# Forgetting attention: logits as three passes over keys and queries split in two parts

## The chip, the cores and the metric

The kernel runs on one core of one Trainium2 chip. The metric is the device time of one execution in microseconds; where several runs are shown it is their median. The profile is of one execution, taken by the hardware profiler, and has its own time.

## The reference, cut to what matters

One layer of a decoder trunk: x is 512 tokens of width 2048, 16 learned tokens go ahead of them, and everything is in float32. One projection makes the inputs of three mixers that work side by side on their own heads: a gated DeltaNet (6 heads of 128), a gated linear attention (5 heads), and the forgetting attention (5 heads of 128) that this document is about. Their outputs, each times a SiLU gate, go through one output projection.

```python
def forgetting_attention(q, k, v, log_f):
    c = jnp.cumsum(log_f, axis=-1)
    ...
    def one_block(args):          # swept in blocks of 128 queries
        i, q_i, c_i = args
        q_pos = i * BLOCK + jnp.arange(BLOCK)
        logits = jnp.einsum('bhqd,bhkd->bhqk', q_i, k) + c_i[..., :, None] - c[:, :, None, :]
        mask = (key_pos[None, :] <= q_pos[:, None]) & (key_pos[None, :] >= PAD)
        probs = jax.nn.softmax(jnp.where(mask, logits, NEG), axis=-1)
        return jnp.einsum('bhqk,bhkd->bhqd', probs, v)
    ...

def hybrid_layer(x, ...):
    proj = (h @ w_in).astype(f32)
    ...
    log_f = jax.nn.log_sigmoid(ff + b_f.astype(f32)).transpose(0, 2, 1)
    o_fox = forgetting_attention(to_heads(fq, FOX_HEADS) * FOX_D ** -0.5, to_heads(fk, FOX_HEADS),
                                 to_heads(fv, FOX_HEADS), log_f)
    o_fox = o_fox.reshape(fz.shape) * jax.nn.silu(fz)
    o = jnp.concatenate([o_dn, o_gla, o_fox], axis=-1)[:, PAD:].astype(x.dtype)
    return x + o @ w_out
```

## The kernel before

Everything is held transposed: 128 columns of a head on the partitions, the T = 528 positions (16 learned tokens, then 512) along the free axis.

**The input projection.** `inproj` makes one block of 128 output columns at a time. The weights come in halves of 128x1024 (`load_half`); each half is split into a high part `hi`, a copy in the type float32r, and a low part `lo`, the rest (L149 on ScalarE, L150 on VectorE). The input is split in the same way into `xh` and `xl`. For each of 16 slices of the contraction L198 issues three passes, hi·xh, hi·xl and lo·xh, into one PSUM bank of 512 columns, or into two of 264 where the 16 learned tokens are wanted too. A product of such split parts is one instruction on TensorE, a product of two float32 tensors is two. The output projection (L992) works in the same three passes.

**A head of the forgetting attention** (`fox_head`). The projections of keys, values, queries and gate are evacuated from PSUM by `evac`, which multiplies by the norm's factor (L316, and L318 for queries, which are scaled too). Keys and queries are float32 and lie in one tile of three rows of 528 columns, `qk`, of which the middle row is unused. Values and probabilities are split into high and low parts; the fourth block of both also has a float32 copy.

Per block b of 128 queries the logits are two products in full precision, with the queries of the block as weights: `pfa` (L903) against the 16 + 128 b positions before the block, `pfd` (L904) against the block itself. So `pfa` has 16, 144, 272 and 400 columns, and `pfd` always 128. VectorE subtracts the forget bias and takes the maximum of each row (L907, L909), ScalarE takes the exponential (L912), VectorE divides by the sum (L913 to L917). TensorE transposes the probabilities (L920, into `pfx`), which are split again (L923, L924). After the fourth block the outputs are accumulated (L936 to L939) and multiplied by the gate (L940).

```python
        for b in range(NB):
            m = NM + b * P
            ts = bsl(b)
            ...
            PE.matmul(pa[:, :m], qT[:, ts], kT[:, :m], start=True, stop=True)
            PE.matmul(pd[:, :P], qT[:, ts], kT[:, ts], start=True, stop=True)
```

**What sets the order.** A scheduler lays out each engine's instructions when the program is built; on the chip every engine takes its own in that order. Between a block's logits and its transposes stand some 50 matmuls of the next projections (of the output projection in the last head), which fill TensorE while softmax runs on VectorE and ScalarE. Buffers that matter here: the pool tag `row` has seven buffers of 128x531 for values, probabilities, gates and the like; `six` has eight of 128x1584 (the tile `qk` is one); the PSUM tag `m` has four banks, shared by logits, transposes and outputs. Loads of weights are issued by SyncE.

Of the kernel before, what the change touches and what calls it, by code (L numbers as in the profile page):

```python
# [8 lines left out]
F32 = mybir.dt.float32  # L9
F32R = mybir.dt.float32r  # L10
# [4 lines left out]
ALU = mybir.AluOpType  # L15
# [3 lines left out]
P = 128  # L19
D = 2048  # L20
KT = D // P
NM = 16
S = 512
T = NM + S
# [53 lines left out]
def tile_hybrid_trunk(ctx, tc, xT, xtok, mtok, w_gate, w_in, w_out, consts, lmask, fin_w, out, dbg=None):  # L78
# [8 lines left out]
    six = pool("six", 8)  # L87
    wk = pool("wk", 2)
# [4 lines left out]
    def row(name, dt=F32):  # L93
        return wk.tile([P, 3 + T], dt, tag="row", bufs=7, name=name)
# [4 lines left out]
    V, A, G, PE = nc.vector, nc.scalar, nc.gpsimd, nc.tensor  # L99
# [93 lines left out]
    def inproj_part(ps, parts, k0, n, hi, lo, m=P):  # L193
        for j in range(n):
            k = k0 + j
            for wt, xx in ((hi, xh), (hi, xl), (lo, xh)):
                for p_, (t0, nt) in zip(ps, parts):
                    mm = PE.matmul(p_[:, :nt], wt[:, j * m : (j + 1) * m], xx[k][:, t0 : t0 + nt],  # L198
                                   start=(k == 0 and wt is hi and xx is xh),
                                   stop=(k == KT - 1 and wt is lo))  # L200
                    order.append(mm.ins)

    def inproj_begin(key, meta=True, first=0):
        b = BLOCK_OF[key]
        n = (T - first) // 2
        parts = [(first, n), (first + n, n)] if meta else [(NM, S)]
        ps = [psb.tile([P, 512], F32, tag="b", name=f"pp{b}_{i}") for i in range(len(parts))]
        return b, ps, parts
# [3 lines left out]
    def inproj(key, meta=True, first=0):  # L212
        if key not in done:
            b, ps, parts = inproj_begin(key, meta, first)
            head[key] = len(order)
            for half in range(2):
                inproj_part(ps, parts, 8 * half, 8, *load_half(w_in[b, half], f"{b}_{half}"))
            done[key] = [(p_[:, :n], t0, n) for p_, (t0, n) in zip(ps, parts)]
        return done.pop(key)
# [91 lines left out]
    def evac(parts, dst, off=0, rows=slice(0, P), scale=None):  # L311

        for p_, t0, n in parts:
            o = dst[rows, off + t0 : off + t0 + n]
            if scale is None:
                V.tensor_tensor(out=o, in0=p_[rows], in1=rstd[rows, t0 : t0 + n], op=ALU.mult)  # L316
            else:
                V.scalar_tensor_tensor(out=o, in0=p_[rows], scalar=scale, in1=rstd[rows, t0 : t0 + n],  # L318
                                       op0=ALU.mult, op1=ALU.mult)
# [29 lines left out]
    for k in range(KT):  # L349
        for xx in (xh, xl):  # L350
            for a in range(2):
                PE.matmul(pgate[a][:, :HT], wg[k // 8][:, k % 8, :], xx[k][:, a * HT : (a + 1) * HT],  # L352
                          start=(k == 0 and xx is xh), stop=(k == KT - 1 and xx is xl))
# [505 lines left out]


    def fox_head(h):
        qk = six.tile([P, 3, T], F32, tag="six", name=f"fqk{h}")
        kT, qT = qk[:, 0], qk[:, 2]
        evac(inproj(("fk", h)), kT)

        v = row(f"vf{h}")[:, :T]
        evac(inproj(("fv", h)), v)
        pv = psm.tile([P, 512], F32, tag="m", name=f"pvf{h}")
        for b in range(NB):
            PE.transpose(pv[:, b * P : (b + 1) * P], v[:, bsl(b)], ident)  # L870
        vhi, vlo = (row(f"v{n}{h}", dt=F32R)[:, :S] for n in ("hi", "lo"))
        v3 = t15(f"v3{h}", (P, P))
        A.copy(vhi, pv)
        V.tensor_tensor(out=vlo, in0=pv, in1=vhi.bitcast(F32), op=ALU.subtract)
        A.copy(v3, pv[:, 3 * P :])
        v4 = t15(f"v4{h}", (P, 2 * NB, NM))
        G.tensor_copy(v4, v[:, 0:NM].unsqueeze(1).to_broadcast([P, 2 * NB, NM]))
        pw = psm.tile([P, 512], F32, tag="m", name=f"pwf{h}")
        PE.transpose(pw[:, :P], v4.rearrange("p b t -> p (b t)"), ident)
        vm = t15(f"fvm{h}", (P, 2, P), F32R)  # L880
        A.copy(vm[:, 0], pw[:, :P])
        V.tensor_tensor(out=vm[:, 1], in0=pw[:, :P], in1=vm[:, 0].bitcast(F32), op=ALU.subtract)
        evac(inproj(("fq", h), meta=False), qT, scale=float(P) ** -0.5)
        cc = six.tile([P, 2 * T + S], F32, tag="six", name=f"fc{h}")
        z = wk.tile([P, S], F32, tag="gd", name=f"fz{h}") if h < 2 else cc[:, T + S : T + 2 * S]
        gate_z("fz", h, z)
        cb, cm = cc[:, :T], cc[:, T : T + S].rearrange("p (b t) -> p b t", b=NB)
        nc.scalar.dma_start(out=cb, in_=gd[12 + h, :].partition_broadcast(P))
        G.affine_select(out=cm, in_=cb[:, NM:].rearrange("p (b t) -> p b t", b=NB), pattern=[[0, NB], [-1, P]],
                        base=0, channel_multiplier=1, compare_op=ALU.is_ge, fill=BIG)  # L890


        mt = t15(f"fmt{h}", (P, NB, 2, NM), F32R)
        pm = row(f"ptm{h}", dt=F32R)[:, :S]
        G.tensor_copy(pm, zero_c.to_broadcast([P, S]))
        hi, lo = (six.tile([P, 3, T], F32R, tag="six", name=f"fp{n}{h}") for n in ("hi", "lo"))
        p3 = t15(f"fp3{h}", (P, P))
        for b in range(NB):
            m = NM + b * P
            ts = bsl(b)  # L900
            pa = psm.tile([P, 512], F32, tag="m", name=f"pfa{h}{b}")
            pd = psm.tile([P, 512], F32, tag="m", name=f"pfd{h}{b}")
            PE.matmul(pa[:, :m], qT[:, ts], kT[:, :m], start=True, stop=True)  # L903
            PE.matmul(pd[:, :P], qT[:, ts], kT[:, ts], start=True, stop=True)  # L904
            pr = row(f"fp{h}{b}")[:, :T]
            sm = wk.tile([P, 4], F32, tag="fsm", name=f"fsm{h}{b}")
            V.tensor_tensor_reduce(out=pr[:, :m], in0=pa[:, :m], in1=cb[:, :m], scale=1.0, scalar=-3e38,  # L907
                                   op0=ALU.subtract, op1=ALU.max, accum_out=sm[:, 0:1])
            V.tensor_tensor_reduce(out=pr[:, m : m + P], in0=pd[:, :P], in1=cm[:, b], scale=1.0, scalar=sm[:, 0:1],  # L909
                                   op0=ALU.subtract, op1=ALU.max, accum_out=sm[:, 1:2])  # L910
            V.tensor_scalar_mul(sm[:, 2:3], sm[:, 1:2], -1.0)
            A.activation(pr[:, : m + P], pr[:, : m + P], AF.Exp, bias=sm[:, 2:3], accum_out=sm[:, 3:4])  # L912
            V.reciprocal(sm[:, 0:1], sm[:, 3:4])  # L913
            V.tensor_scalar_mul(mt[:, b, 0], pr[:, :NM], sm[:, 0:1])
            V.scalar_tensor_tensor(out=mt[:, b, 1], in0=pr[:, :NM], scalar=sm[:, 0:1],
                                   in1=mt[:, b, 0].bitcast(F32), op0=ALU.mult, op1=ALU.subtract)
            V.tensor_scalar_mul(pr[:, NM : m + P], pr[:, NM : m + P], sm[:, 0:1])  # L917
            px = psm.tile([P, 512], F32, tag="m", name=f"pfx{h}{b}")
            for jb in range(b + 1):
                PE.transpose(px[:, jb * P : (jb + 1) * P], pr[:, NM + jb * P : NM + (jb + 1) * P], ident)  # L920
            n = min(b + 1, 3)
            x, bs = px[:, : n * P].rearrange("p (j t) -> p j t", j=n), slice(b * P, (b + 1) * P)
            A.copy(hi[:, :n, bs], x)  # L923
            V.tensor_tensor(out=lo[:, :n, bs], in0=x, in1=hi[:, :n, bs].bitcast(F32), op=ALU.subtract)  # L924
            if b == 3:
                A.copy(p3, px[:, 3 * P :])
        pw = psm.tile([P, 512], F32, tag="m", name=f"pfw{h}")
        PE.transpose(pw[:, :P], mt.bitcast(F32).rearrange("p b i t -> p (b i t)"), ident)
        for b in range(NB):
            r, bs = slice(32 * b, 32 * b + 32), slice(b * P, (b + 1) * P)  # L930
            A.copy(pm[r, bs], pw[r, :P])
        po = psm.tile([P, 512], F32, tag="m", name=f"pfo{h}")
        for jb in range(3):
            js, qs = slice(jb * P, (jb + 1) * P), slice(jb * P, S)
            for i, (v_, p_) in enumerate(((vhi, hi), (vhi, lo), (vlo, hi))):
                PE.matmul(po[:, qs], v_[:, js], p_[:, jb, qs], start=(jb + i == 0), stop=False)  # L936
        PE.matmul(po[:, 3 * P :], v3, p3, start=False, stop=False)
        for i in range(2):
            PE.matmul(po, vm[:, i], pm, start=False, stop=i == 1)  # L939
        V.tensor_tensor(out=z, in0=po[:, :512], in1=z, op=ALU.mult)  # L940
# [89 lines left out]
    for cc in range(4):  # L1030
# [6 lines left out]
        pa = [psb.tile([P, 512], F32, tag="b", name=f"pa{cc}{tb}") for tb in range(4)]  # L1037
# [20 lines left out]
    for c in range(4):  # L1058
        f = part(f"fw{c}").bitcast(F32)
# [86 lines left out]
```

## Time and profile before

| what | value |
|---|---|
| median of 3 runs | 1019.95 us (1019.50 to 1020.04) |
| the profiled execution's own time | 1018.81 us |
| its span, first to last instruction | 1017.1 us |
| mean granted TensorE clock | 0.998 |
| TensorE busy | 1006.3 us, 99% |
| VectorE busy | 558.2 us, 55% |
| ScalarE busy | 416.5 us, 41% |
| GpSimd busy | 135.5 us, 13% |

PE is TensorE's matmuls, PEld its loads of weights, DVE VectorE, ACT ScalarE, POOL GpSimd, SP SyncE. A row of the order of time has the start and the length in us, the engine, the line, the operation, what is written from what, the shape (weights, then the moving operand) and how many instructions in a row are merged. Matmuls overlap, so their lengths do not add up; from start to start they do. A row of grouped instructions has the count, then busy time in us, the mean length of one in ns, and the engine's idle time ahead of them with what ended it. A row of waits has the total in us, how many, and the longest. Both types of operand, float32 and its split parts, are shown as f32 in matmul rows.

### The profile page before, as it was taken

What the parts mean: (1) busy time and instruction counts of PE and PEld (TensorE: products, weight loads), DVE (VectorE), ACT (ScalarE), POOL (GpSimd) and SP (SyncE); (2) the same over time, 40 slices, a digit from 0 to 9 for tenths busy, and PEclk for the clock granted to TensorE, in tenths of its full rate; (3) what the DMA queues carried; (4) which work ended last, traced back from release to release, by engine and by line L of the source; (5) the groups of instructions that cost most, each with busy time, mean ns of one, the idle gap of its engine ahead of it and who ended that gap; (6) DMA issues with size and microseconds to landing.
All of it is one profiled execution on the core that took longest, in us unless ns stands there. A gap on an engine that the chain in (4) does not pass through costs nothing.

```text
span 1017.1 us, 18766 instructions
## 1 busy us (share of the span) xinstructions
PE 1006.3 (99%) x7662; PEld 907.4 (89%) x7662; DVE 558.2 (55%) x1226; ACT 416.5 (41%) x916; POOL 135.5 (13%) x141
## 2 busy tenths in 40 slices
PE   9999999999999999999999999999999999999996
PEld 8899999899999888998999979898989888888885
DVE  6376867856566984343838373544444474323333
ACT  7653533443456333344544434333333362223224
POOL 0021411211112221100110021010101000000014
PEclk9999999999999999999999999999999999999999
DMA  9623133233221333222122222322223263232244
GB/s 356 221 68 131 65 99 105 83 100 104 91 79 64 98 104 100 71 79 70 63 65 69 67 92 63 94 92 70 92 82 92 85 204 128 83 104 90 96 145 166
DMA packets 42410, 105.03 MB, mean 103 GB/s; under 512 B 10733, under 2 KB 13981, under 8 KB 42324
## 3 DMA queue, kind: packets, MB, share of 16 engines
q1 hardware_dynamic: 28064, 92.23, 27.3%
q10 hardware_dynamic: 14260, 11.61, 4.1%
q8 instruction: 60, 0.98, 0.4%
q14 instruction: 26, 0.21, 0.1%
HBM read 98.64 MB, written 5.05 MB: 102 GB/s over the span
## 4 chain that ended last, share of the span: by engine, by line
PE 92%; DVE 3%; ACT 2%; DMA 1%; POOL 1%; issue 1%; ACTq 1%; DVEq 0%; POOLq 0%
PE pp L198 57%; PE pa L992 16%; PE pp L252 4%; PE pss L773 1%; POOL stgz L325 1%; PE pgate L352 1%; PE pfo L936 1%; PE pfa L903 1%; DVE ot L507 1%; DVE wlo L150 1%; PE pg L474 1%; PE pa L615 1%; PE py L639 1%; DMA sc<-ab 1%; PE pb L992 1%
## 5 line engine op out<-in xcount | busy, mean ns | idle before, releaser
L198 PE MATMUL pp<-xl,whi 128*128 128x264 f32 (+2 forms) x1456 | 378.6, 310 | 0.0
L198 PE MATMUL pp<-xh,whi 128*128 128x264 f32 (+2 forms) x1456 | 376.1, 310 | 0.1
L198 PE MATMUL pp<-xh,wlo 128*128 128x264 f32 (+2 forms) x1456 | 375.2, 309 | 0.4 <-DVE wlo L150 0.4
L198 PEld LDWEIGHTS pp<-xl,whi 128*128 128x128 f32 x1456 | 244.4, 189 | 13.6 <-issue 0.2
L198 PEld LDWEIGHTS pp<-xh,wlo 128*128 128x128 f32 x1456 | 243.6, 188 | 14.2 <-DVE wlo L150 0.9
L198 PEld LDWEIGHTS pp<-xh,whi 128*128 128x128 f32 x1456 | 243.0, 188 | 14.5 <-issue 0.8
L149 ACT CAST whi<-raw 128x1024 fp32r<-128x1024 f32 x110 | 115.4, 1049 | 201.5 <-PE pp L198 159.8
L150 DVE TENSOR_TENSOR wlo<-raw,whi 128x1024 fp32r<-128x1024 f32 x110 | 134.6, 1224 | 108.5 <-ACT whi L149 98.2
L992 PE MATMUL pa<-whio,ol 128*128 128x512 f32 x224 | 88.1, 393 | 0.0
L992 PE MATMUL pa<-wloo,oh 128*128 128x512 f32 x224 | 88.0, 393 | 0.0
L150 DVE TENSOR_TENSOR wloo<-rawo,whio 128x1024 fp32r<-128x1024 f32 x29 | 35.9, 1236 | 81.2 <-ACT whio L149 81.2
L992 PE MATMUL pa<-whio,oh 128*128 128x512 f32 x224 | 78.0, 396 | 0.0
L149 ACT CAST whio<-rawo 128x1024 fp32r<-128x1024 f32 x29 | 30.4, 1050 | 83.7 <-PE pa L992 65.1
L992 PEld LDWEIGHTS pa<-whio,ol 128*128 128x128 f32 x224 | 42.1, 188 | 9.8
L992 PEld LDWEIGHTS pa<-wloo,oh 128*128 128x128 f32 x224 | 42.1, 188 | 9.4
L992 PEld LDWEIGHTS pa<-whio,oh 128*128 128x128 f32 x224 | 41.9, 188 | 9.2
L325 POOL TENSOR_SCALAR stc<-cv 128x528 f32<-128x528 f32 (+1 forms) x18 | 28.2, 1564 | 138.3 <-DVE cv L409 115.3
L409 DVE SCALAR_TENSOR_TENSOR cv<-pb,cpk,cv 128x528 f32<-128x528 f32 (+1 forms) x54 | 40.8, 755 | 0.7
L1019 POOL TENSOR_TENSOR acc<-acc,fw 128x512 f32<-128x512 f32 x12 | 15.7, 1349 | 159.1 <-DMA fw<-in_fin_w 159.1
L316 DVE TENSOR_TENSOR pb<-pp,rstd 128x264 f32<-128x264 f32 (+1 forms) x36 | 13.7, 422 | 23.3 <-PE pp L198 23.3
L507 DVE TENSOR_TENSOR ot<-ab 51x30 f32<-51x30 f32 (+14 forms) x60 | 21.2, 354 | 3.6 <-DMA ab<-scmeta 2.1
L325 POOL TENSOR_SCALAR stfz<-zfz 128x512 f32<-128x512 f32 x5 | 9.8, 1965 | 99.0 <-ACT whi L149 49.0
(391 smaller groups left out, 1285.4 us busy)
## 6 DMA issues: line engine op xcount, KB each, us to landing
raw<-in_w_in SPq DMA_DIRECT2D x110, 512.0 KB, 3.3
rawo<-in_w_out SPq DMA_DIRECT2D x29, 512.0 KB, 3.3
xt<-in_xtok SPq DMA_DIRECT2D x8, 512.0 KB, 9.8
acc<-in_xtok ACTq DMA_DIRECT2D x16, 256.0 KB, 5.1
out<-acc SPq DMA_DIRECT2D x16, 256.0 KB, 3.0
xs<-in_xT SPq DMA_DIRECT2D x7, 528.0 KB, 6.7
gb<-gd ACTq DMA_DIRECT2D x2, 792.0 KB, 6.1
eg<-gd ACTq DMA_DIRECT2D x8, 192.0 KB, 3.4
```

The source lines that it names most:

```text
L149: A.copy(hi, raw)
L150: V.tensor_tensor(out=lo, in0=raw, in1=hi.bitcast(F32), op=ALU.subtract)
L198: mm = PE.matmul(p_[:, :nt], wt[:, j * m : (j + 1) * m], xx[k][:, t0 : t0 + nt], start=(k == 0 and wt is hi and xx is xh), stop=(k == KT - ...
L252: mm = PE.matmul(ps[:, :S], wt[:, j * P : (j + 1) * P], xx[k][:, NM:T], start=(k == 0 and wt is hi and xx is xh), stop=(k == KT - 1 and wt ...
L316: V.tensor_tensor(out=o, in0=p_[rows], in1=rstd[rows, t0 : t0 + n], op=ALU.mult)
L325: G.tensor_scalar_max(t, src, LOW)
L352: PE.matmul(pgate[a][:, :HT], wg[k // 8][:, k % 8, :], xx[k][:, a * HT : (a + 1) * HT], start=(k == 0 and xx is xh), stop=(k == KT - 1 and ...
L409: V.scalar_tensor_tensor(out=c, in0=pb[:, t0 + w : w + T], scalar=cwc[:, blk, w : w + 1], in1=c, op0=ALU.mult, op1=ALU.add)
L474: PE.matmul(pg[:r, j * r : (j + 1) * r], kT[:, j, ts], kT[:, j, ts], start=True, stop=True)
L507: V.tensor_tensor(out=t3, in0=a3[:, j + 1 :, j : j + 1].to_broadcast([NN * 4 + H, m, j]), in1=a3[:, j : j + 1, 0:j].to_broadcast([NN * 4 + ...
L992: PE.matmul(p_, o_[:, s], w_, start=(first and n == 0), stop=(last and n == 2), **kw)
L1019: G.tensor_tensor(out=acc[tb, cc], in0=acc[tb, cc], in1=fw[cc], op=ALU.mult)
```

## The change

Keys and queries are each written first into a float32 buffer `kf` of which there is one, shared by both. From there ScalarE copies the high part in float32r and VectorE makes the low part. High and low keys and high queries take the three rows of `qk`; the queries' low part takes a `row` buffer. Each of the two products of a block becomes three passes accumulated in PSUM: high queries with high keys, high queries with low keys, low queries with high keys; the passes of `pfa` and `pfd` alternate. The product of the two low parts is left out.

```diff
     def fox_head(h):
-        qk = six.tile([P, 3, T], F32, tag="six", name=f"fqk{h}")
-        kT, qT = qk[:, 0], qk[:, 2]
-        evac(inproj(("fk", h)), kT)
+        qk = six.tile([P, 3, T], F32R, tag="six", name=f"fqk{h}")
+        kh, kl, qh = (qk[:, i] for i in range(3))
+        kf = wk.tile([P, T], F32, tag="kf", bufs=1, name=f"kf{h}")
+        evac(inproj(("fk", h)), kf)
+        A.copy(kh, kf)
+        V.tensor_tensor(out=kl, in0=kf, in1=kh.bitcast(F32), op=ALU.subtract)
...
-        evac(inproj(("fq", h), meta=False), qT, scale=float(P) ** -0.5)
+        qf = wk.tile([P, T], F32, tag="kf", bufs=1, name=f"qf{h}")
+        ql = row(f"ql{h}", dt=F32R)[:, :T]
+        evac(inproj(("fq", h), meta=False), qf, scale=float(P) ** -0.5)
+        A.copy(qh[:, NM:], qf[:, NM:])
+        V.tensor_tensor(out=ql[:, NM:], in0=qf[:, NM:], in1=qh[:, NM:].bitcast(F32), op=ALU.subtract)
...
-            PE.matmul(pa[:, :m], qT[:, ts], kT[:, :m], start=True, stop=True)
-            PE.matmul(pd[:, :P], qT[:, ts], kT[:, ts], start=True, stop=True)
+            for i, (q_, k_) in enumerate(((qh, kh), (qh, kl), (ql, kh))):
+                PE.matmul(pa[:, :m], q_[:, ts], k_[:, :m], start=i == 0, stop=i == 2)
+                PE.matmul(pd[:, :P], q_[:, ts], k_[:, ts], start=i == 0, stop=i == 2)
```

## The prediction

> **What bounds the kernel now.** I read the page first (busy shares, then the chain that ended last), then the busy times by window over the five attention heads, then TensorE's order of time around the logits.
>
> ```profile
> span 1017.1 us, 18766 instructions
> PE 1006.3 (99%) x7662; PEld 907.4 (89%) x7662; DVE 558.2 (55%) x1226; ACT 416.5 (41%) x916; POOL 135.5 (13%) x141
> PE 92%; DVE 3%; ACT 2%; DMA 1%; POOL 1%; issue 1%; ACTq 1%; DVEq 0%; POOLq 0%
> sum 236.00, PE 235.95 PEld 207.82 DVE 118.22 ACT 85.69 POOL 14.51; mean PE 47.19 PEld 41.56 DVE 23.64 ACT 17.14 POOL 2.90
> ```
>
> The last line sums five windows, 634 to 870 us, one for each head's logits and what stands among them. TensorE is busy in 235.95 of 236.00 us there, VectorE in half, ScalarE in a third. So in this stage time is what TensorE's instructions take, one behind the other; what the change adds elsewhere costs nothing as long as TensorE does not come to wait for it.
>
> The durations of matmuls overlap, so I price them by start to start. These are the logits of head 0, block by block (`pfa`: keys before the block, `pfd`: the block itself); the projection's matmuls (L198) follow.
>
> ```profile
> 634.25 0.29 PE L903 MATMUL pfa<-fqk 128*128 128x16 f32 x2
> 634.39 0.47 PE L904 MATMUL pfd<-fqk 128*128 128x128 f32 x2
> 634.62 0.37 PE L198 MATMUL pp<-xl,whi 128*128 128x264 f32 x1
> 634.82 0.30 PE L198 MATMUL pp<-xh,wlo 128*128 128x264 f32 x1
> ...
> 639.45 0.41 PE L903 MATMUL pfa<-fqk 128*128 128x144 f32 x2
> 639.84 0.37 PE L198 MATMUL pp<-xh,whi 128*128 128x264 f32 x1
> 640.04 0.29 PE L198 MATMUL pp<-xl,whi 128*128 128x264 f32 x1
> ...
> 649.14 0.62 PE L903 MATMUL pfa<-fqk 128*128 128x272 f32 x2
> 649.75 0.48 PE L198 MATMUL pp<-xh,whi 128*128 128x512 f32 x1
> 650.06 0.39 PE L198 MATMUL pp<-xl,whi 128*128 128x512 f32 x1
> 650.30 0.40 PE L198 MATMUL pp<-xh,wlo 128*128 128x512 f32 x1
> ...
> 657.58 0.84 PE L903 MATMUL pfa<-fqk 128*128 128x400 f32 x2
> 658.39 0.48 PE L198 MATMUL pp<-xh,wlo 128*128 128x512 f32 x1
> 658.71 0.39 PE L198 MATMUL pp<-xh,whi 128*128 128x512 f32 x1
> 658.94 0.40 PE L198 MATMUL pp<-xl,whi 128*128 128x512 f32 x1
> ```
>
> A full-precision product is two instructions (x2 in every `pfa` row), a product of split parts one. The first L198 after a full-precision pair starts early and is long by what the pair still takes, so I end a block at the start of the second L198, less one ordinary step of L198: 0.12 us at 264 columns, 0.23 at 512 (658.71 to 658.94).
>
> Block 0: 634.82 - 0.12 - 634.25 = 0.45 us. Block 1: 640.04 - 0.12 - 639.45 = 0.47. Block 2: 650.06 - 0.23 - 649.14 = 0.69. Block 3: 658.71 - 0.23 - 657.58 = 0.90. Together 2.51 us for a head, **12.5 us for five**. That is all the change can win: 1.2% of the span.
>
> **What a narrow pass costs.** No row of this trace shows a product of split parts with fewer than 256 columns. A head gets 24 passes, six a block; 18 of them are under that: the 12 of `pfd` (128 columns) and the six of `pfa` in blocks 0 and 1 (16 and 144). Only six are wide (272 and 400). So the price of a narrow pass decides. The nearest row is of four full-precision products, two instructions each, with almost no columns:
>
> ```profile
> 494.56 0.95 PE L738 MATMUL psd<-half_c,gpr 128*128 128x2 f32 x8
> 495.37 0.36 PE L198 MATMUL pp<-xl,whi 128*128 128x264 f32 x1
> 495.57 0.28 PE L198 MATMUL pp<-xh,wlo 128*128 128x264 f32 x1
> 495.69 0.28 PE L198 MATMUL pp<-xh,whi 128*128 128x264 f32 x1
> L903 PEld LDWEIGHTS pfa<-fqk x40: 187/190/192, 634.1 to 854.0; 128*128 128x128 f32 x40
> L198 PEld LDWEIGHTS pp<-xh,whi x1456: 186/188/193, 60.3 to 824.7; 128*128 128x128 f32 x182
> ```
>
> Eight instructions that stream two columns each take 495.57 - 0.12 - 494.56 = 0.89 us, **0.111 us apiece**: with 128x128 weights to load for every matmul, the load and not the columns sets the step. Block 0 says the same: 0.45 us for four instructions, two with 16 columns and two with 128. The last two rows show a load of a full-precision operand at 190 ns and of a split part at 188 ns, so I take the same 0.111 us for a pass of split parts however narrow. Bounds: from below the streaming alone, (0.231 - 0.122)/248 = 0.00044 us a column and 0.006 on top, which gives 0.062 us at 128 columns; from above the whole full-precision product of that width, 0.22 us. I stay at 0.111 because the equal load rows are the nearest.
>
> The Trainium skill (TensorE: Matmul & The Clock Gate, LDWEIGHTS) puts a load at columns/1.2 ns, an estimate of 107 ns for 128 columns; the trace has 111. By that figure the sum below would be +1.7 us and not +2.1; the measured one decides.
>
> **The change part by part.**
> *Logits on TensorE.* Six passes a block in place of two products. A wide pass follows L198's line: 0.122 + 8 x 0.00044 = 0.126 us at 272 columns, 0.182 at 400; each hides the next load.
> Block 0: 6 x 0.111 = 0.67 us (+0.22). Block 1: 0.67 (+0.20). Block 2: 3 x 0.126 + 3 x 0.111 = 0.71 (+0.02). Block 3: 3 x 0.182 + 3 x 0.111 = 0.88 (-0.02). A head: 2.93 against 2.51, +0.42. **Five heads: +2.1 us**, all on the path. So the change trades two slow streams for three weight loads, and three quarters of the passes are too narrow to gain from streaming. If a load could run further ahead under a wide neighbour, blocks 2 and 3 would take 0.67 and 0.73 and the sum be +1.1 us.
>
> *Splits of keys and queries.* Each head gains two ScalarE copies and two VectorE subtractions; the evacuations stay, into another buffer.
>
> ```profile
> L985 DVE TENSOR_TENSOR ol<-zsgz,oh 128x512 fp32r<-128x512 f32 x5 | 3.1, 684 | 0.0
> L984 ACT CAST oh<-zsgz 128x512 fp32r<-128x512 f32 x5 | 2.8, 617 | 0.8 <-DVE ol L985 0.8
> ```
>
> By these two rows: 2 x 0.69 = 1.4 us of VectorE and 2 x 0.62 = 1.2 us of ScalarE a head, 7 and 6 us in all, beside engines with 118 and 150 us free in the 236. I cost them at nothing. What covers them: the operand is made long before it is used. The closest case before is the last head:
>
> ```profile
> 814.33 0.69 DVE L318 SCALAR_TENSOR_TENSOR fqk<-pp,rstd 128x512 f32<-128x512 f32 x1 [2.62 <-PE pp L198]
> 815.22 1.23 DVE L150 TENSOR_TENSOR wlo<-raw,whi 128x1024 fp32r<-128x1024 f32 x1 [0.20 <-ACT whi L149]
> 820.26 0.29 PE L903 MATMUL pfa<-fqk 128*128 128x16 f32 x2
> ```
>
> The queries are ready at 815.02, their first use is at 820.26: 5.2 us for a copy (0.6), a weight subtraction queued ahead (1.2) and the subtraction (0.7), 2.5 in all. Without that cover it would cost 1.3 us a head.
>
> *New waits.* Each subtraction waits for its copy on ScalarE. The query evacuation shares one buffer with the keys, so it also waits for the keys' subtraction, and the next head's keys for the queries'; those stand ahead of it on VectorE itself in the built program's order, so that wait is over by the time it comes up. Queued behind a subtraction on VectorE stands a weight subtraction (L150), behind a copy on ScalarE a weight cast (L149), and TensorE waits for those. They have room:
>
> ```profile
> ACT whi L149 <- PE pp L198: 42.7, 19, 5.8
> DVE wlo L150 <- ACT whi L149: 48.9, 29, 5.6
> ```
>
> From 560 to 880 us the casts themselves waited 42.7 us for TensorE to release a buffer: the weights are made as soon as there is room, up to 5.8 us early.
>
> *Softmax.* The part that takes TensorE's result and brings it back for the transposes has its least margin in head 3, block 0:
>
> ```profile
> 778.61 0.28 DVE L917 TENSOR_SCALAR fp<-fp,fsm 128x128 f32<-128x128 f32 x1
> 780.31 0.27 PE L920 MATMUL pfx<-ident,fp 128*128 128x128 f32 x1
> ...
> 686.11 0.35 DVE L917 TENSOR_SCALAR fp<-fp,fsm 128x256 f32<-128x256 f32 x1
> 689.00 0.38 PE L920 MATMUL pfx<-ident,fp 128*128 128x128 f32 x2
> ```
>
> The probabilities are ready at 778.89, wanted at 780.31: 1.4 us. More usual is head 1, block 1: 689.00 - 686.46 = 2.5 us. The built order keeps about 50 L198 between logits and transposes, as before; the last pass ends 0.2 us later, and one subtraction more may stand in the way: 0.9 us, still under 1.4.
>
> *Rows and banks.* The queries' low part holds one of the seven row buffers through a head, and PSUM banks are held 0.2 us longer; the order of TensorE's other work is the same but for shifts of a few matmuls. At nothing, bounded by the third rival.
>
> Sum: the profiled execution took 1018.81 us (span 1017.1 and 1.7 around it); with +2.1 it is 1020.9. The median of the runs shown, 1019.95, lies 1.1 above that execution, so the forecast as a median is **1022.1 us**.
>
> **The rivals.**
> *A narrow pass runs at streaming speed.* Then the load of a split part hides where that of a full-precision one does not: blocks of 0.23 (3 x 0.013 + 3 x 0.062 by the line of streaming), 0.39, 0.56 and 0.73 us, 1.91 a head, -0.60, five heads -3.0: **1016.9 us**, faster. It decides once a load of a split part takes under about 0.09 us. For it: nothing but that no row shows a narrow pass. Against it: the equal load rows. The Trainium skill (TensorE: Matmul & The Clock Gate, Weight-path perf modes) has a fast weight load for 128 weights whose type is not FP32, measured at about twice the speed; if it counted the split parts as such, this rival would hold. The equal 188 and 190 ns speak against it.
> *A narrow pass costs what the full-precision product of that width costs.* Three products for one in blocks 0 and 1 and for every `pfd`: (6 x 0.22 - 0.45) + (3 x 0.25 + 3 x 0.22 - 0.47) + (3 x 0.126 + 3 x 0.22 - 0.69) + (3 x 0.182 + 3 x 0.22 - 0.90) = 0.87 + 0.94 + 0.35 + 0.31 = 2.5 a head, +12.4: **1032.3 us**. For it: no row excludes a slow mode under 256 columns. Against it: in the built program a pass is one matmul and one load (40 more in all, 120 for 80), where the full-precision product is two of each, and wide passes run at one column for 0.00044 us.
> *The cover runs out.* A weight subtraction (1.23) and a split (0.69) ahead of a softmax step make 1.9 us where head 3's block 0 has 1.4: about 0.4 us late there, and if five of the twenty blocks were as tight, +2 on top of +2.1: **1024.1 us**. Speaks for it: that block. Against: the 2.5 us of the other row shown, which would cover it all.
>
> **How the numbers follow.** Forecast 0.71, streaming 0.07, full price 0.12, cover 0.10. 0.2% of 1019.95, about what a measurement of this kernel can tell from no change, is 2.04 us: the forecast lies on that edge, so of its 0.71 I put 0.42 above and 0.29 within. Slower 0.42 + 0.12 + 0.10 = 0.64, same 0.29, faster 0.07. The range holds the forecast and the third rival, 8 in 10: from 1020.6 (+1.1 with loads running ahead, less half a microsecond) to 1026.0 (the third rival with the stall twice as long).
>
> **What would show it.** Right: `pfd` and narrow `pfa` passes at steps of 0.11 us, blocks at 0.67, 0.67, 0.71 and 0.88 us, L198 and the rest unchanged, TensorE still without idle time in the five heads. Wrong: steps of 0.06 or of 0.22 at 128 columns; an idle gap of TensorE ahead of a transpose or of a logit pass with the splits as releaser; a shift of time outside the heads.

## The result, and the profile after

The changed kernel takes 1021.4 us, the median of 19 runs (1020.09 to 1023.59), and the kernel before 1019.5 us in 19 runs (1018.29 to 1021.55). The ratio is 1.0019 with a 95% interval of 1.0012 to 1.0026: **slower by 1.9 us**, which is little, but the interval leaves out no change. The profiled execution after took 1021.69 us. Below are its span, the busy times and the shares of the chain that ended last, from the page.

```profile
span 1020.0 us, 18860 instructions
PE 1008.4 (99%) x7702; PEld 911.6 (89%) x7702; DVE 566.9 (56%) x1236; ACT 422.0 (41%) x926; POOL 132.6 (13%) x141
PE 97%; ACT 1%; issue 0%; DVE 0%; DMA 0%; ACTq 0%; SPq 0%; DVEq 0%
```

TensorE has 40 matmuls and 40 loads more (7662 before) and is 2.1 us longer busy (1006.3 before). VectorE and ScalarE are busy 8.7 and 5.5 us longer, at 56% and 41%. The chain that ended last runs over TensorE for 97% of the span (92% before). The sum over five windows, 634 to 872 us, one for each head's logits and what stands among them:

```profile
sum 238.00, PE 238.00 PEld 211.92 DVE 123.73 ACT 90.41 POOL 14.10; mean PE 47.60 PEld 42.38 DVE 24.75 ACT 18.08 POOL 2.82
```

TensorE is busy in all 238.00 us. Its waits between 600 and 880 us are an empty list, so nothing that was added on the other engines stopped it there, and what the change costs in this stretch has to lie in TensorE's own instructions. These are blocks 0 to 3 of head 0 in TensorE's order of time, with the transpose ahead of each and the second L198 behind it (`pfa` is now L911, `pfd` L912):

```profile
633.86 0.27 PE L882 MATMUL pwf<-ident,v 128*128 128x128 f32 x1
633.88 0.26 PE L911 MATMUL pfa<-fqk 128*128 128x16 f32 x1
633.99 0.31 PE L912 MATMUL pfd<-fqk 128*128 128x128 f32 x1
634.13 0.23 PE L911 MATMUL pfa<-fqk 128*128 128x16 f32 x1
634.22 0.31 PE L912 MATMUL pfd<-fqk 128*128 128x128 f32 x1
634.36 0.23 PE L911 MATMUL pfa<-fqk,ql 128*128 128x16 f32 x1
634.44 0.31 PE L912 MATMUL pfd<-fqk,ql 128*128 128x128 f32 x1
634.58 0.34 PE L198 MATMUL pp<-xh,whi 128*128 128x264 f32 x1
634.76 0.28 PE L198 MATMUL pp<-xl,whi 128*128 128x264 f32 x1
...
639.40 0.27 PE L928 MATMUL pfx<-ident,fp 128*128 128x128 f32 x1
...
640.30 0.28 PE L198 MATMUL pp<-xl,whi 128*128 128x264 f32 x1
...
648.90 0.38 PE L928 MATMUL pfx<-ident,fp 128*128 128x128 f32 x2
649.03 0.37 PE L911 MATMUL pfa<-fqk 128*128 128x272 f32 x1
649.24 0.22 PE L912 MATMUL pfd<-fqk 128*128 128x128 f32 x1
649.30 0.34 PE L911 MATMUL pfa<-fqk 128*128 128x272 f32 x1
649.48 0.23 PE L912 MATMUL pfd<-fqk 128*128 128x128 f32 x1
649.54 0.34 PE L911 MATMUL pfa<-fqk,ql 128*128 128x272 f32 x1
...
650.06 0.40 PE L198 MATMUL pp<-xl,whi 128*128 128x512 f32 x1
...
657.23 0.49 PE L928 MATMUL pfx<-ident,fp 128*128 128x128 f32 x3
...
658.67 0.40 PE L198 MATMUL pp<-xh,whi 128*128 128x512 f32 x1
```

The first pass is recorded 0.02 us after the transpose ahead of it. Before, a transpose took its usual step there:

```profile
634.14 0.27 PE L879 MATMUL pwf<-ident,v 128*128 128x128 f32 x1
```

to the first product at 634.25, that is 0.11 us. So I count from the transpose and take 0.11 us off for each (two merged in block 2, three in block 3); the end is, as in the prediction, the second L198 less one ordinary step. Block 0: 634.76 - 0.12 - 633.86 - 0.11 = 0.67 us. Block 1: 640.30 - 0.12 - 639.40 - 0.11 = 0.67. Block 2: 650.06 - 0.23 - 648.90 - 0.22 = 0.71. Block 3: 658.67 - 0.23 - 657.23 - 0.33 = 0.88. Measured in this way over all twenty blocks, the logits take 14.83 us after and 12.60 before: **+2.23 us**. From the start of the first `pfa` to the start of the last matmul of the output projection it is 373.19 us before and 375.16 after, +1.97. The stretch after holds one L198 more (0.12 us), so like for like it is +1.85; where the 0.4 us between this and the blocks' sum go is not found.

The loads of the weights show the price of a pass without any such correction. These are some of block 0's, in the order of time of PEld:

```profile
633.86 0.19 PEld L911 LDWEIGHTS pfa<-fqk 128*128 128x128 f32 x1
633.97 0.19 PEld L912 LDWEIGHTS pfd<-fqk 128*128 128x128 f32 x1
...
634.52 0.19 PEld L198 LDWEIGHTS pp<-xh,whi 128*128 128x128 f32 x1
```

Six loads start one 0.11 us behind the other, 634.52 - 633.86 = 0.66 us in all, whether 16 columns follow or 128. The record of a load is 0.19 us long, so two neighbours overlap in the records; what a pass costs is the step.

### The profile page after: what moved, and what is told of

The parts are those of the page before. It is cut to its first block, busy times and chain, and to the rows that moved or that the text cites. A ratio compares the mean times of both kernels' runs of the same rounds, so it can differ in the third digit from the quotient of the medians.

```text
span 1020.0 us, 18860 instructions
## 1 busy us (share of the span) xinstructions
PE 1008.4 (99%) x7702; PEld 911.6 (89%) x7702; DVE 566.9 (56%) x1236; ACT 422.0 (41%) x926; POOL 132.6 (13%) x141
## 4 chain that ended last, share of the span: by engine, by line
PE 97%; ACT 1%; issue 0%; DVE 0%; DMA 0%; ACTq 0%; SPq 0%; DVEq 0%
PE pp L198 63%; PE pa L1000 16%; PE pp L252 4%; PE pss L773 1%; PE pgate L352 1%; PE pfo L944 1%; PE pfa L911 1%; PE pg L474 1%; PE pfd L912 1%; PE pa L615 1%; PE pb L1000 1%; PE py L639 1%; PE pfx L928 1%; PE po L654 1%; PE po L653 1%; PE pks L632 1%
## 5 line engine op out<-in xcount | busy, mean ns | idle before, releaser
L198 PE MATMUL pp<-xl,whi 128*128 128x264 f32 (+2 forms) x1456 | 377.9, 310 | 0.0
L198 PE MATMUL pp<-xh,whi 128*128 128x264 f32 (+2 forms) x1456 | 376.0, 310 | 0.1
L198 PE MATMUL pp<-xh,wlo 128*128 128x264 f32 (+2 forms) x1456 | 375.0, 309 | 0.0
L198 PEld LDWEIGHTS pp<-xl,whi 128*128 128x128 f32 x1456 | 244.2, 189 | 13.4 <-issue 0.2
L198 PEld LDWEIGHTS pp<-xh,whi 128*128 128x128 f32 x1456 | 243.2, 188 | 14.3 <-issue 0.6
L198 PEld LDWEIGHTS pp<-xh,wlo 128*128 128x128 f32 x1456 | 243.6, 188 | 13.4 <-issue 0.2
```

## The experiments

My theory was that a pass with few columns costs the load of its weights, 0.11 us, whatever its width. Against it stood: streaming speed for narrow passes, a price that grows with the width, loads that run further ahead under a wide neighbour, and a part of the time that is the splits' and not the passes'. Each ratio is against the kernel before on the same chip, whose median was 1019.50 us for the changed kernel, 1019.88 for the first four experiments and 1020.01 for the other three; an experiment had 5 to 11 runs. "Logits" are the twenty blocks as above; "section" is the stretch from the first `pfa` to the last matmul of the output projection.

| kernel | us | ratio (95%) | logits, us | section, us |
|---|---|---|---|---|
| before | | 1 | 12.60 | 373.19 |
| after | 1021.40 | 1.0019 (1.0012 to 1.0026) | 14.83 | 375.16 |
| one pass | 1012.95 | 0.9928 (0.9916 to 0.9941) | 5.04 | 365.60 |
| padded | 1022.55 | 1.0025 (1.0014 to 1.0036) | 14.84 | 375.50 |
| splits only | 1021.13 | 1.0010 (1.0001 to 1.0018) | 12.60 | 373.23 |
| merged, three passes | 1016.86 | 0.9967 (0.9955 to 0.9979) | 10.07 | 370.64 |
| merged, full precision | 1018.25 | 0.9985 (0.9976 to 0.9994) | 11.38 | 371.95 |
| grouped | 1021.55 | 1.0019 (1.0010 to 1.0028) | 14.69 | 375.10 |
| passes only | 1021.61 | 1.0016 (1.0007 to 1.0025) | 14.78 | 375.35 |

**One pass.** The changed kernel with the first of the three passes alone.

```diff
-            for i, (q_, k_) in enumerate(((qh, kh), (qh, kl), (ql, kh))):
-                PE.matmul(pa[:, :m], q_[:, ts], k_[:, :m], start=i == 0, stop=i == 2)
-                PE.matmul(pd[:, :P], q_[:, ts], k_[:, ts], start=i == 0, stop=i == 2)
+            PE.matmul(pa[:, :m], qh[:, ts], kh[:, :m], start=True, stop=True)
+            PE.matmul(pd[:, :P], qh[:, ts], kh[:, ts], start=True, stop=True)
```

> The changed kernel with only the first of the three logit passes (high queries with high keys); the two correction passes are left out of the computation, the splits are still made. My theory (a pass of under 256 columns costs one load of 128x128 weights, 0.112 us, a wide one its columns; splits cost nothing): blocks of 0.22, 0.22, 0.24 and 0.29 us, 4.9 us for five heads against 12.6 before: 7.7 us less than before (ratio 0.9925). Rival A (the 2 us of the change come from the splits on VectorE and ScalarE, the six passes cost what the two products cost): 12.6/3 = 4.2 us of passes and 2 us of stalls, 6.4 us less (0.9937). Rival B (the first pass pays something that the later ones do not): under 6 us less.

Block 0 of head 0 in its order of time:

```profile
634.24 0.27 PE L882 MATMUL pwf<-ident,v 128*128 128x128 f32 x1
634.26 0.26 PE L910 MATMUL pfa<-fqk 128*128 128x16 f32 x1
634.38 0.31 PE L911 MATMUL pfd<-fqk 128*128 128x128 f32 x1
634.52 0.34 PE L198 MATMUL pp<-xh,whi 128*128 128x264 f32 x1
634.69 0.28 PE L198 MATMUL pp<-xl,whi 128*128 128x264 f32 x1
```

634.69 - 0.12 - 634.24 - 0.11 = 0.22 us for two passes, 0.11 each. The 80 passes that the changed kernel has more cost it 14.83 - 5.04 = 9.79 us; the prediction's prices (60 narrow at 0.111, ten at 0.126, ten at 0.182) make 9.74. In the section they are worth 9.56 us, and by the ratios 9.3 us of the kernel's time (1.0019 - 0.9928). So a microsecond of passes is about a microsecond of the kernel: nothing hides them. The time alone would not part this from the rival in which the splits cost 2 us, since 0.9937 lies in the interval; the blocks do, with 5.04 us of passes where that rival has 4.2, and TensorE has no wait from 600 to 880 us.

**Padded.** The changed kernel with `pfa` of blocks 0 and 1 widened from 16 and 144 columns to 240.

```diff
+            w = max(m, 240)
...
-                PE.matmul(pa[:, :m], q_[:, ts], k_[:, :m], start=i == 0, stop=i == 2)
+                PE.matmul(pa[:, :w], q_[:, ts], k_[:, :w], start=i == 0, stop=i == 2)
```

> The changed kernel with the narrow passes over the keys ahead of the block (16 and 144 columns) widened to 240 columns; the added columns are not read. My theory (the load sets the step): the same blocks of 0.67 and 0.67 us, the same time as the changed kernel, 1.9 us above before (1.0019). Rival C (load and streaming add up): 3 x 224 and 3 x 96 columns of 0.00044 us a head, +2.1 us for five heads on top, 1.0040.

Block 0 of head 0:

```profile
635.25 0.27 PE L882 MATMUL pwf<-ident,v 128*128 128x128 f32 x1
635.28 0.36 PE L912 MATMUL pfa<-fqk 128*128 128x240 f32 x1
635.47 0.23 PE L913 MATMUL pfd<-fqk 128*128 128x128 f32 x1
...
636.16 0.28 PE L198 MATMUL pp<-xl,whi 128*128 128x264 f32 x1
```

636.16 - 0.12 - 635.25 - 0.11 = 0.68 us, against 0.67 with 16 columns; all logits 14.84 us against 14.83. Fifteen times the columns at the same time: up to 240 columns the width is free, and something that each pass has once sets the step. That rules out both rivals that price a narrow pass by its width. The intervals of this kernel and of the changed one overlap.

That would be so too if every matmul had a fixed price, whatever its weights. No run here tries that, but a row of the kernel before speaks against it, six full-precision products of another mixer with 64x64 weights:

```profile
231.03 0.91 PE L557 MATMUL pn<-uf,an 64*64 64x64 f32 x12
231.87 0.39 PE L198 MATMUL pp<-xl,whi 128*128 128x264 f32 x1
232.10 0.40 PE L198 MATMUL pp<-xh,wlo 128*128 128x264 f32 x2
```

Measured as the eight two-column instructions of the prediction were, 232.10 - 0.12 - 231.03 = 0.95 us for twelve, 0.079 apiece and not 0.111, though each streams 64 columns and not two. What is smaller is the weights, so I put the step down to their load.

**Splits only.** The kernel before, with the copies and subtractions of keys and queries added and their results unused.

```diff
         evac(inproj(("fk", h)), kT)
+        sp = wk.tile([P, T], F32R, tag="kf", bufs=1, name=f"kh{h}")
+        ql = row(f"ql{h}", dt=F32R)[:, :T]
+        A.copy(sp, kT)
+        V.tensor_tensor(out=ql, in0=kT, in1=sp.bitcast(F32), op=ALU.subtract)
...
         evac(inproj(("fq", h), meta=False), qT, scale=float(P) ** -0.5)
+        sq = wk.tile([P, T], F32R, tag="kf", bufs=1, name=f"qh{h}")
+        A.copy(sq[:, NM:], qT[:, NM:])
+        V.tensor_tensor(out=ql[:, NM:], in0=qT[:, NM:], in1=sq[:, NM:].bitcast(F32), op=ALU.subtract)
```

> The kernel before with the splits of keys and queries added (both copies and both subtractions a head) and not used: the logits stay full-precision products. My theory: VectorE +7 us busy, ScalarE +6 us, TensorE's order covers both: 1.0000, within 0.05%. Rival A (the splits cost the 2 us): 1.0019.

This missed what I expected: it came out 1.2 us above the kernel before (1021.13 - 1019.88), a ratio of 1.0010, with an interval that just leaves out 1. The logits are as before, 12.60 us, and so is the section to 0.04 us. One new wait of TensorE in the heads can be named:

```profile
642.03 0.28 PE L198 MATMUL pp<-xh,wlo 128*128 128x264 f32 x1
642.76 0.47 PE L198 MATMUL pp<-xh,whi 128*128 128x512 f32 x1 [0.44 <-DVE fqk L316]
```

VectorE evacuates the keys late, and the projection waits 0.44 us for the bank. The section does not show it because this build's order has four L198 fewer in it, about 0.5 us. The changed kernel has no such wait. The other 0.8 us would lie outside the section. There TensorE waits in other mixers' work: from 60 to 634 us 2.2 us in all here, 1.6 before and 0.8 after. But it waits 2.8 us there in "passes only", below, which has no splits at all, and the start of the first L198 alone moved by 1.1 us between the profiles of before (60.38) and after (61.46). So such differences ahead of the heads come without splits too, and this experiment does not settle what the splits cost in the changed kernel; "passes only" asks that directly.

**Merged, three passes.** The changed kernel with `pfa` and `pfd` as one pass in blocks 0 to 2 (the positions lie side by side), and block 3 cut into two equal halves of 264 columns (`HT`). VectorE's maximum of block 3 is taken in three steps for that.

```diff
-                PE.matmul(pa[:, :m], q_[:, ts], k_[:, :m], start=i == 0, stop=i == 2)
-                PE.matmul(pd[:, :P], q_[:, ts], k_[:, ts], start=i == 0, stop=i == 2)
+                if b < 3:
+                    PE.matmul(pa[:, : m + P], q_[:, ts], k_[:, : m + P], start=i == 0, stop=i == 2)
+                else:
+                    PE.matmul(pa[:, :HT], q_[:, ts], k_[:, :HT], start=i == 0, stop=i == 2)
+                    PE.matmul(pd[:, :HT], q_[:, ts], k_[:, HT:], start=i == 0, stop=i == 2)
```

> The changed kernel with the two products of a block made one: the keys ahead of the block and those of the block lie side by side, so blocks 0 to 2 have three passes of 144, 272 and 400 columns in one bank, and block 3 three times two passes of 264 in two banks (one more maximum on VectorE there). Half the loads in blocks 0 to 2 go. My theory: blocks of 0.34, 0.38, 0.55 and 0.73 us, 1.99 a head, 10.0 us for five against 12.6 before and 14.8 after: 2.6 us less than before (0.9974). Rival A: the splits' 2 us stay, 0.6 us less than before (0.9994). Rival D (the third maximum in block 3 delays the transposes by 0.4 us a head): 0.9994 too, with an idle gap of TensorE ahead of the transposes.

Block 0 of head 0:

```profile
634.93 0.27 PE L882 MATMUL pwf<-ident,v 128*128 128x128 f32 x1
634.96 0.42 PE L912 MATMUL pfa<-fqk 128*128 128x144 f32 x2
635.22 0.28 PE L912 MATMUL pfa<-fqk,ql 128*128 128x144 f32 x1
635.33 0.33 PE L198 MATMUL pp<-xh,whi 128*128 128x264 f32 x1
635.50 0.28 PE L198 MATMUL pp<-xl,whi 128*128 128x264 f32 x1
```

635.50 - 0.12 - 634.93 - 0.11 = 0.34 us, half of 0.67: three loads in place of six, the same columns. This version is 0.33% faster than the kernel before (0.9967, 3.0 us between the medians) and the fastest here that keeps all three passes; by the ratios it beats the changed kernel by 0.52%, some 5 us.

**Merged, full precision.** The same merging in the kernel before: what merging gives without the change.

```diff
-            PE.matmul(pa[:, :m], qT[:, ts], kT[:, :m], start=True, stop=True)
-            PE.matmul(pd[:, :P], qT[:, ts], kT[:, ts], start=True, stop=True)
+            if b < 3:
+                PE.matmul(pa[:, : m + P], qT[:, ts], kT[:, : m + P], start=True, stop=True)
+            else:
+                PE.matmul(pa[:, :HT], qT[:, ts], kT[:, :HT], start=True, stop=True)
+                PE.matmul(pd[:, :HT], qT[:, ts], kT[:, HT:], start=True, stop=True)
```

> The kernel before (full-precision logits, no splits) with the two products of a block made one as in the merged three-pass kernel: 144, 272 and 400 columns in one bank, block 3 twice 264. My theory: the two instructions of a full-precision product stream 0.00084 us a column each and cost a load at least: blocks of 0.25, 0.46, 0.68 and 0.90 us, 2.28 a head, 11.4 us for five against 12.6: 1.1 us less than before (0.9989), and 1.4 to 2 us more than the merged three-pass kernel. Rival E (what the merged three-pass kernel won came from the merge alone, by one VectorE step's place or a bank that is free earlier, not from the passes): 0.9967 here too.

Block 0 of head 0:

```profile
635.49 0.41 PE L904 MATMUL pfa<-fqk 128*128 128x144 f32 x2
635.64 0.38 PE L198 MATMUL pp<-xl,whi 128*128 128x264 f32 x1
635.86 0.28 PE L198 MATMUL pp<-xh,wlo 128*128 128x264 f32 x1
```

635.86 - 0.12 - 635.49 = 0.25 us, where the two products took 0.45. Four full-precision instructions, 0.45 us, have become two of 0.12: the product had been held by its loads too, and at 144 columns its own streaming is just above them. The ratio's interval leaves out the 0.9967 of the merged three-pass kernel, so the merge alone does not explain that one. Merging is worth 1.2 us of logits here (12.60 to 11.38) and 4.8 in three passes (14.83 to 10.07). The change therefore has its sign by how the products are cut: on the kernel as it was, it costs 2.2 us of logits, on the merged one it gains 11.38 - 10.07 = 1.3. By the ratios the gain is 0.0018, with about 0.0015 of uncertainty.

The two merged kernels also price one product at a time, in head 0 by the same measure: three passes against full precision take 0.34 against 0.25 us at 144 columns, 0.38 against 0.46 at 272, 0.54 against 0.68 at 400, and 0.74 against 0.90 for twice 264.

**Grouped.** The changed kernel with all passes of `pfa` first and then all of `pfd`, instead of alternating.

```diff
-            for i, (q_, k_) in enumerate(((qh, kh), (qh, kl), (ql, kh))):
+            passes = ((qh, kh), (qh, kl), (ql, kh))
+            for i, (q_, k_) in enumerate(passes):
                 PE.matmul(pa[:, :m], q_[:, ts], k_[:, :m], start=i == 0, stop=i == 2)
+            for i, (q_, k_) in enumerate(passes):
                 PE.matmul(pd[:, :P], q_[:, ts], k_[:, ts], start=i == 0, stop=i == 2)
```

> The changed kernel with the passes in another order: the three over the keys ahead of the block, then the three over the block itself, instead of in turn. My theory (every pass pays its own load, no load runs further ahead than one pass): the same blocks of 0.67, 0.67, 0.72 and 0.89 us, 1.0022 as the changed kernel. Rival F (changing the bank at every pass costs): shorter blocks 0 and 1, by more than 0.05 us each. Rival G (loads run ahead under wide passes): blocks 2 and 3 change, 0.67 and 0.73.

Logits 14.69 us against 14.83, the ratio the same 1.0019. Blocks 0 and 1 stay at 0.67 us, so changing the bank at every pass costs nothing that shows. Whether a narrow pass has a wide neighbour makes 0.14 us in a hundred and twenty passes: a load does not run ahead under a wide pass by enough to pay for the next narrow one.

**Passes only.** The changed kernel without its splits: keys and queries are evacuated straight into the high parts, and all three passes take those. It leaves out the low parts, and its logits are three times the product of the high ones; only its time is of use.

```diff
-        evac(inproj(("fk", h)), kf)
-        A.copy(kh, kf)
-        V.tensor_tensor(out=kl, in0=kf, in1=kh.bitcast(F32), op=ALU.subtract)
+        evac(inproj(("fk", h)), kh)
...
-            for i, (q_, k_) in enumerate(((qh, kh), (qh, kl), (ql, kh))):
+            for i, (q_, k_) in enumerate(((qh, kh), (qh, kh), (qh, kh))):
```

> The changed kernel without the copies, the subtractions and the shared buffer: keys and queries are evacuated into their high parts and all three passes take these, so the low parts are left out of the computation. My theory: TensorE's blocks unchanged at 0.67, 0.67, 0.72 and 0.89 us, 14.8 us for five heads, 1.0019 to 1.0022. Rival A (of the change's 1.9 us one comes from the splits, as the run with the splits alone may say): 1.0010.

1021.61 us, logits 14.78: the changed kernel's time without a single split. On the same chip "grouped", which has the splits, took 1021.55. The passes alone make the whole loss that is measured; the splits' share, by the ratios, is 0.0003, some 0.3 us, with about 1.1 us of uncertainty to either side (the two intervals' half-widths, 0.0007 and 0.0009, combined), so it is not told from nothing.

## Why the prediction was right

**TensorE bounds the heads.** Right: 238.00 of 238.00 us busy, and in the section "one pass" gives back 9.56 us for 9.79 us of passes.

**The price of a narrow pass.** The step on which the sign hung. The prediction took 0.111 us from eight instructions of two columns, between bounds of 0.062 and 0.22. Measured: 0.67 us for six passes in block 0, 0.111 to 0.112 each, the same at 16, 128, 144 and 240 columns. The Trainium skill (TensorE: Matmul & The Clock Gate, LDWEIGHTS) says that a load's time goes by the columns of the weights, at columns/1.2 ns, which gives an estimate of 107 ns for 128. The trace agrees in that up to 240 streamed columns do not enter, and the measured step is 4% longer.

**The blocks.** 0.67, 0.67, 0.71 and 0.88 us were worked out, and the four blocks of head 0 measure 0.67, 0.67, 0.71 and 0.88. The sum over five heads is +2.23 us in the traces where +2.1 was given; the section shows +1.97 and the medians +1.9, with about 0.7 us of uncertainty to either side, so that the medians come within 0.2 us of +2.1 is in part luck.

**Outside the heads.** A shift of time there was named as a sign of being wrong, and the two profiled executions do differ there. After, the first L198 starts 1.1 us later, the stretch from it to the first `pfa` is 1.5 us shorter (573.88 and 572.42), and what lies behind the section is 1.3 us longer. The same stretch takes 575.44 us in "passes only", the changed kernel without its splits. With one profile of each I read this as scatter, and not as the change; that is not shown.

**Loads running ahead** (the low end of the range, +1.1). Wrong in both tests: in block 2 the starts of the three wide passes lie 649.30 - 649.03 = 0.27 (with what the transposes left over) and 649.54 - 649.30 = 0.24 us apart, which is 0.126 + 0.111 for a wide and a narrow pass, the load's full price. And "grouped", without the alternation, came out the same.

**The rivals.** Streaming speed would have given 0.23 us in block 0, full price three times 0.45: neither is near 0.67. With the first rival falls the reading that the fast weight load of the Trainium skill (TensorE: Matmul & The Clock Gate, Weight-path perf modes) takes in these split parts. The group of the weight loads of the logits after, with least, median and longest of one in ns, is where it would show:

```profile
L911 PEld LDWEIGHTS pfa<-fqk x40: 187/189/192, 633.9 to 856.1; 128*128 128x128 f32 x40
```

189 ns, with 190 for the full-precision operand before: no load became faster.

**The cover.** Held. The splits are these two groups of VectorE and two of ScalarE (count, busy us, mean ns, idle ahead):

```profile
L867 DVE TENSOR_TENSOR fqk<-kf,fqk 128x528 fp32r<-128x528 f32 x5 | 3.5, 703 | 0.0
L890 DVE TENSOR_TENSOR ql<-qf,fqk 128x512 fp32r<-128x512 f32 x5 | 3.4, 683 | 0.0
L866 ACT CAST fqk<-kf 128x528 fp32r<-128x528 f32 x5 | 3.2, 635 | 0.0
L889 ACT CAST fqk<-qf 128x512 fp32r<-128x512 f32 x5 | 3.1, 616 | 0.0
```

6.9 and 6.3 us, as costed, and none of them appears in a wait of TensorE anywhere in the execution. The weight casts still run early; from 560 to 880 us they waited for TensorE, 43.2 us in all and up to 4.7 at a time.

Softmax kept its room. The tightest block is now head 2's block 0:

```profile
726.56 0.28 DVE L925 TENSOR_SCALAR fp<-fp,fsm 128x128 f32<-128x128 f32 x1
...
728.31 0.27 PE L928 MATMUL pfx<-ident,fp 128*128 128x128 f32 x1
```

Ready at 726.84, wanted at 728.31: 1.47 us, where the least before was 1.4. Between logits and transposes stand 32 to 57 matmuls (32 to 56 before), where I had put some 50. The rival that let this cover run out asked for a stall ahead of a transpose, and there is none. Its sum had a slip as well: 1.9 less 1.4 is 0.5 us late and not 0.4, which would have made it 1024.6 us, still in the range. "Splits only" does show that a build with the splits can lose its cover at one place (0.44 us at 642.76), so "at nothing" holds for the order that the changed kernel was built in, not for every order.

**The absolute time.** 1022.1 us was forecast and 1021.4 came. Of the 0.7 us, 0.45 is the base: the kernel before measured 1019.5 in these 19 runs and 1019.95 in the three shown.

## What to carry to other kernels

Where every matmul brings its own 128x128 weights, count loads first and columns second: on this kernel a pass of up to 240 columns costs 0.111 us however narrow it is. So three narrow passes in place of a full-precision product, which is two instructions, lose at 144 columns and below, and gain at 264 and above. An estimate of the width where they break even is some 200 columns: three loads make 0.33 us, and the two instructions together stream a column in about 0.0017 us, (0.68 - 0.46)/128. Merge products that share their weights and lie side by side before splitting them into passes: the same change was a loss of 2.2 us of logits on the kernel as it was and a gain of 1.3 on the merged one. And look for a row of the old trace whose operation is as starved of columns as the new one; the eight two-column instructions of another mixer priced a narrow pass to 1%.

## What was not expected

The full-precision product, of two instructions, meets the same floor of loads: 16 and 128 columns as two products took 0.45 us, and the same 144 columns as one product 0.25. That made merging worth 1.2 us of logits with no split at all.

In the records, the first pass of split parts stands 0.02 to 0.03 us behind the transpose ahead of it, where a full-precision product stood 0.11 us behind. What is missing there appears again before the next L198, so a block that is measured from its own first start reads 0.08 us too long (0.75 for 0.67). The starts of the matmuls of a block alternate, 0.14 and 0.09 us apart in block 0; those of their loads are even, at 0.11.
